# Ordering 28 experts by their row counts: sorting keys with the eight-maximum instruction

## The chip, the cores and the metric

The kernel runs on one core of a Trainium2 chip. The metric is device time in microseconds (us) of one execution of the whole program; a lower time is better. Engines are named as in the profile: PE is TensorE (PEld its weight loads), DVE is VectorE, ACT is ScalarE, POOL is GpSimd, SP is the sync engine, which issues the large transfers from HBM.

## What is computed

One decoder block over 512 rows of 1024 values: a mixer (retention heads and differential attention heads, merged by gates, one output projection), then a mixture of 32 experts, then a final normalisation. The part that matters here is the mixture:

```python
gp = softmax(h @ w_rg + b_rg);  g_top, g_idx = top_k(gp, 1)
el = (h @ w_re + b_re) of the chosen group of 8
e_val, e_idx = top_k(el, 2)
weights = g_top * softmax(e_val);  expert = g_idx * 8 + e_idx
y[expert] = (silu(x @ w1[e]) * (x @ w3[e])) @ w2[e]
out = sum over the two experts of weights * y
```

Every row has two experts, and how many rows an expert has depends on the data. Each expert has three weight matrices of 2 MB each, all of which are read from HBM.

## The kernel before, in words

The program first does the mixer, then the router (which ends in the counts of rows of each expert, the tile `cnts`), then the experts. The experts' stage takes the experts in units of 128 row slots (`BLOCKS`, in the order `UNITS`). The first four experts (`NFIX`) are taken by number: units 0 and 1 are experts 0 and 1, then 2 and 3. The other 28 are taken by place in a list sorted by number of rows, since an expert with many rows gets more slots than one with few. The list, `order`, holds the expert's number at each place. The inverse, `place`, holds each expert's place; the gathers of rows use it through `pcode`, and `block_list` uses it to list rows that found no slot.

Weights come through `load_in` (gate and up matrices, eight transfers of 512 KB, line 662) and `load_down` (four transfers, line 670), all issued by SP in program order. Each goes into a buffer of a ring of 36, so a transfer waits on SP until the matmuls that read the buffer's last contents are through; whatever stands behind it on SP waits too. For an expert that is taken from the list, SP first reads the expert's number from `order` into a register (line 1373) and waits for it there.

At the end of the router, lines 1150 to 1164, the order of the instructions on every engine is the program's own (`manual_schedule`). ACT copies the counts (line 1153). DVE then works out the last chunk's slot codes and one-hot matrix, the row factors (`factors`, lines 993 and 995) and, after PE's products, the second half of the gathered rows (`scaled`, line 1010). `turn` transposes the gathered rows on PE and scales them into `xT`, the first four blocks on ACT (line 1038) and the last four on DVE (line 1035). After that come `exps` and `weights`, short DVE instructions that make each row's weight in `aux`. Then expert 0's matmuls (`Expert.unit`, line 1222) run.

In the experts' stage only PE's order is fixed by the program. The other engines' instructions are placed by a planner, which estimates when each can start. `run_experts` calls `order_experts` by its hook after expert 0's matmuls have been put down: the whole ordering is DVE work that stands there among the products of the activations (line 1227), the one-hot matrices of the next gather (lines 976 and 978) and the short instructions of `sides` (lines 1043 to 1051). `order_experts` makes keys, compares all 28 with all 28 in a table of 784 values per partition and sums its rows to `place` (lines 1292 and 1295). From `place` it makes `order` with a second table: compare with the numbers of the places (line 1298), multiply by the experts' numbers (line 1300), sum (line 1301), convert (line 1302). The rest moves the row codes to the new places (lines 1304 to 1315). `block_list` (lines 1322 to 1361) is some fifty further short DVE instructions.

`Gather.unit` (lines 1012 to 1023) makes the next unit's rows between the matmuls of an expert; its products on PE (line 1000) wait for the one-hot chunk of line 978.

Of the kernel before, what the change touches and what calls it, by code (L numbers as in the profile page):

```python
# [7 lines left out]
F32 = mybir.dt.float32  # L8
F32R = mybir.dt.float32r
BF16 = mybir.dt.bfloat16  # L10
I32 = mybir.dt.int32
U32 = mybir.dt.uint32
AF = mybir.ActivationFunctionType
ALU = mybir.AluOpType
AX = mybir.AxisListType
# [3 lines left out]
P = 128  # L19
# [5 lines left out]
NEXP = 32  # L25
# [4 lines left out]
NFIX = 4  # L30
# [89 lines left out]
def block_kernel(tc, a, out):  # L120
    nc = tc.nc
    vec, act, pe, pool = nc.vector, nc.scalar, nc.tensor, nc.gpsimd

    def left(name, bufs=1):
        return open_pool(tc, name, bufs, side="left", reuse_waits="tile")

    def right(name, bufs=1):
        return open_pool(tc, name, bufs, side="right", reuse_waits="tile")
# [3 lines left out]
    cp, cp_close = left("consts")  # L132
# [185 lines left out]
    def run(it):  # L318
        for _ in it:
            pass  # L320

    def merged(*its):
        its = list(its)
        while its:
            its = [it for it in its if next(it, 0) is None]
            yield
# [13 lines left out]
    with tc.manual_schedule():  # L340
# [54 lines left out]
        for j in range(NJ):  # L395
            n, k0 = START_STEPS[j], k0s[j]
# [31 lines left out]
            order = [(0, b, m) for m in range(3) for b in range(4)] + [(1, b, m) for b in range(3) for m in range(3)]  # L428
# [337 lines left out]
    rt, rt_close = right("router")  # L766
# [27 lines left out]
    iotae = cst[:, C_IOTAE:C_IOTAE + NEXP]  # L794
# [12 lines left out]
    def router_bias():  # L807
        ps = pm.tile([P, S], F32, name="ps")
        pe.matmul(ps[:, 0:36], onef, wsum, start=True, stop=True)
        vec.tensor_add(br, br, ps[:, 0:36])  # L810
# [5 lines left out]
    vec.memset(gl, -3e38)  # L816
    cnts = cp.tile([P, NEXP], F32, name="cnts")
    efs = cp.tile([P, NT, 2], F32, name="efs")
    Ms = [rt.tile([P, NEXP], BF16, name=f"M{i}") for i in range(NT)]
    for i in range(NT):  # L820
        vec.tensor_scalar(aux[:, i, 0:1], cst[:, C_PIDX:C_PIDX + 1], float(i * P), None, op0=ALU.add)
# [7 lines left out]
    def sm_(name, cols=1, dt=F32):  # L829
        keep = {"s1": 4, "gs": 4, "den": 4, "wx": 4, "g8": 3, "e8": 3, "oh": 3, "rj": 1, "el": 1}  # L830
        return rt.tile([P, cols], dt, name=name, bufs=keep.get(name, 2))

    class Chunk:
# [115 lines left out]
        def weights(self):  # L949
            i = self.i  # L950
            vec.tensor_copy(aux[:, i, 1:2], efs[:, i, 0:1])
            vec.tensor_mul(self.den, self.den, self.gs)
            vec.reciprocal(self.den, self.den)
            vec.tensor_scalar(self.wx, self.wx, self.den, None, op0=ALU.mult)
            vec.tensor_copy(aux[:, i, 2:4], self.wx)
            vec.tensor_sub(aux[:, i, 4:6], self.wx, aux[:, i, 2:4].bitcast(F32))

    def g_tile():
        return gp.tile([P, NT, P], F32R, name="G")

    def row_tile():
        return gp.tile([P, KD, P], F32, name="xT")
# [122 lines left out]
    with tc.manual_schedule():  # L1085
        ch = [Chunk(i) for i in range(NT)]
        g0 = Gather(dcode, aux, cst[:, C_CBASE:C_CBASE + 2 * CAP], cst[:, C_ESLOT:C_ESLOT + 1],
                    lambda: pm.tile([P, S], F32, name="ps"), lambda: pm.tile([P, S], F32, name="ps"), g_tile())
        for i in range(NT):
            c, b, d = ch[i], ch[i - 1] if i else None, ch[i - 2] if i > 1 else None  # L1090
            c.project(0)
            c.project(1)
            if b:
                b.turn(1)
                b.logits(0)
                b.logits(1)
            c.turn(0)
            if d:
                d.count()
                run(d.codes())  # L1100
                d.exps()
            c.square(0)
            c.split(0)
            if i == NT - 1:
                c.logits(0)
            c.project(2)
            if b:
                b.turn_logits()
                b.split(1)
            if d:  # L1110
                d.factor()
                run(g0.build_chunk(d.i))
            c.project(3)
            if i == 0:
                router_bias()
            c.residual(2 if i == NT - 1 else 1)
            if i < NT - 1:
                c.square(1)
            if b:
                run(b.choose())  # L1120
        pss = [pj.tile([P, S], F32, name="pj") for _ in range(2)]
        b, c = ch[NT - 2:]

        def gather(i, *nhs):
            for nh in nhs:
                g0.product(pss[nh], i, nh)
                if nh:
                    g0.side_product(i, FACTOR)

        gather(0, 0, 1)  # L1130
        c.turn(1)
        c.square(1)
        c.logits(1)
        c.split(1)
        b.count()
        c.turn_logits()
        gather(1, 0, 1)

        def rest():
            yield from b.codes()  # L1140
            yield from g0.build_chunk(b.i)
            b.factor()
            yield
            c.factor()
            yield
        run(merged(c.choose(), rest()))
        gather(b.i, 0)
        c.count()
        gather(b.i, 1)
        pc = pm.tile([P, S], F32, name="ps")  # L1150
        for q in range(NT):
            pe.matmul(pc[:, 0:NEXP], oneb, Ms[q], start=(q == 0), stop=(q == NT - 1))
        act.copy(cnts, pc[:, 0:NEXP])
        run(c.codes())
        run(g0.build_chunk(c.i))
        g0.side_product(c.i, FACTOR)
        for nh in range(2):
            g0.product(pss[nh], c.i, nh)
            if nh == 0:
                g0.factors()  # L1160
            g0.scaled(pss[nh], nh)
        g0.turn(row_tile())
        b.exps()
        c.exps()
        act.activation(lame, ones.to_broadcast([P, 2]), AF.Silu)
        for c in ch:
            c.weights()
# [10 lines left out]
    mk, mk_close = right("moe")  # L1178
# [100 lines left out]


    place = mk.tile([P, NEXP], F32, name="place")
    order = mk.tile([P, NEXP], I32, name="order")
    pcode = cp.tile([P, 2, NT], F32, name="pcode")
    paux = cp.tile([P, NT, 8], F32R, name="paux")

    def order_experts():
        n = NEXP - NFIX
        key = mk.tile([P, NEXP], F32, name="key")
        vec.scalar_tensor_tensor(key, cnts, -float(NEXP), iotae, op0=ALU.mult, op1=ALU.add)
        t = mk.tile([P, D], F32, name="yt", bufs=1)  # L1290
        c = t[:, 0:n * n].rearrange("p (a b) -> p a b", a=n)
        vec.tensor_tensor(c, key[:, NFIX:, None].to_broadcast([P, n, n]),
                          key[:, None, NFIX:].to_broadcast([P, n, n]), op=ALU.is_gt)
        vec.tensor_copy(place[:, 0:NFIX], iotae[:, 0:NFIX])
        vec.reduce_sum(place[:, NFIX:], c, axis=AX.X)
        vec.tensor_scalar(place[:, NFIX:], place[:, NFIX:], float(NFIX), None, op0=ALU.add)

        vec.tensor_tensor(c, place[:, None, NFIX:].to_broadcast([P, n, n]),
                          iotae[:, NFIX:, None].to_broadcast([P, n, n]), op=ALU.is_equal)
        vec.tensor_mul(c, c, iotae[:, None, NFIX:].to_broadcast([P, n, n]))  # L1300
        vec.reduce_sum(key[:, NFIX:], c, axis=AX.X)
        vec.tensor_copy(order[:, NFIX:], key[:, NFIX:])

        vec.tensor_sub(key, place, iotae)
        c = t[:, 0:2 * NT * NEXP].rearrange("p (a b) -> p a b", a=2 * NT)
        ef = efs.rearrange("p i k -> p (i k)")
        vec.tensor_tensor(c, ef[:, :, None].to_broadcast([P, 2 * NT, NEXP]),
                          iotae[:, None, :].to_broadcast([P, 2 * NT, NEXP]), op=ALU.is_equal)
        vec.tensor_mul(c, c, key[:, None, :].to_broadcast([P, 2 * NT, NEXP]))
        mv = mk.tile([P, NT, 2], F32, name="mv")  # L1310
        vec.reduce_sum(mv.rearrange("p i k -> p (i k)"), c, axis=AX.X)
        for k in range(2):
            vec.scalar_tensor_tensor(pcode[:, k, :], mv[:, :, k], 512.0, dcode[:, k, :], op0=ALU.mult, op1=ALU.add)
        vec.tensor_copy(paux, aux.bitcast(F32))
        vec.tensor_add(paux[:, :, 1], efs[:, :, 0], mv[:, :, 0])
# [172 lines left out]
    def hook(e):  # L1488
        if e == 0:
            order_experts()  # L1490
        if e == 6:
            block_list()
# [59 lines left out]
```

## Time and profile before

| what | value |
|---|---|
| time, median of 3 runs (lowest, highest) | 1133.92 us (1133.46, 1135.08) |
| the profiled execution: its own time, its span | 1135.46 us, 1133.7 us |
| mean granted TensorE clock in it | 0.989 of full speed |
| busy share of the span: PE, PEld, DVE, ACT, POOL | 95%, 59%, 55%, 30%, 7% |
| moved by DMA | 284.02 MB, mean 251 GB/s |
| experts' stage (first expert's matmuls to last weights landed) | about 640 to 1115 us of the span |

The busy shares are means over stages with different limits: in the mixer PE leads, in the experts' stage the weights' transfers occupy the DMA engines nearly all the time. A change in the middle of the program is therefore read from the stretch it lies in. A "form" such as 128x784 gives partitions and elements per partition.

### The profile page before, as it was taken

To read this page: it belongs to the slowest core of one execution; us is meant where nothing else is said; L and a number is where in the kernel's file an instruction comes from. 1 tells how busy PE (TensorE), PEld (TensorE's weight loads), DVE (VectorE), ACT (ScalarE), POOL (GpSimd) and SP (SyncE) were. 2 spreads that over 40 slices of the span, in tenths; PEclk is the share of its full clock that TensorE was granted. 3 is DMA by queue.
4 is the path that set the end of the run, shared out by engine and by line. 5 is a ranking of instruction groups with operands and counts; after the bars stand their busy time and mean duration, and the time that the engine had idled before them with its cause. 6 is when DMAs were issued, how large, how long until landed. Compare 5 with 4: busy or idle time off the path is not lost.

```text
span 1133.7 us, 15015 instructions
## 1 busy us (share of the span) xinstructions
PE 1071.7 (95%) x5178; PEld 665.0 (59%) x5178; DVE 622.2 (55%) x1443; ACT 338.4 (30%) x701; POOL 79.0 (7%) x106
## 2 busy tenths in 40 slices
PE   5999999999999999999999899999999999999885
PEld 3777778778788776788877444444432443234222
DVE  3468667644445765655775765755442553244244
ACT  4553233333343534444334211111111110111123
POOL 1031000000021111000013100000000000000001
PEclk9999999999999999999999999999999999999998
DMA  9945645622323221244286899999999999999994
GB/s 317 274 149 186 222 132 185 204 76 81 105 82 105 75 74 39 75 151 146 91 278 235 302 373 391 391 400 393 391 392 400 392 391 391 400 393 394 389 397 159
DMA packets 139889, 284.02 MB, mean 251 GB/s; under 512 B 10977, under 2 KB 34585, under 8 KB 139681
## 3 DMA queue, kind: packets, MB, share of 16 engines
q1 hardware_dynamic: 136656, 281.29, 68.6%
q10 hardware_dynamic: 3152, 1.73, 0.6%
q8 instruction: 42, 0.69, 0.3%
q14 instruction: 39, 0.31, 0.1%
HBM read 280.88 MB, written 2.11 MB: 250 GB/s over the span
## 4 chain that ended last, share of the span: by engine, by line
PE 67%; DMA 19%; DVE 7%; ACT 2%; issue 2%; POOL 1%; SPq 0%; ACTq 0%; DVEq 0%; POOLq 0%
PE pj L209 31%; PE gu L1222 12%; DMA ew<-in_w_exp_up_dram 9%; DMA ew<-in_w_exp_down_dram 5%; PE py L1242 5%; PE pa L1000 4%; PE pa L1269 4%; DMA wa<-in_w_ada_dram 3%; PE pj L391 2%; PE ps L485 2%; PE ps L695 1%; DMA wst<-in_w_in_dram 1%; DVE acc L462 1%; PE ps L391 1%; DVE qk L448 1%
## 5 line engine op out<-in xcount | busy, mean ns | idle before, releaser
L1222 PE MATMUL gu<-ew,xT 128*64 128x512 f32 (+1 forms) x1088 | 222.4, 601 | 12.6 <-DMA ew<-in_w_exp_gate_dram 8.4
L209 PE MATMUL pj<-ew,whi 128*128 128x512 f32 x512 | 168.2, 410 | 0.0
L164 DVE TENSOR_TENSOR wlo<-wst,whi 128x1024 fp32r<-128x1024 f32 x79 | 100.0, 1267 | 87.0 <-ACT whi L163 79.5
L209 PE MATMUL pj<-whi,ew 128*128 128x512 f32 x384 | 131.0, 409 | 2.8 <-DVE v L480 2.8
L1222 PEld LDWEIGHTS gu<-ew,xT 128*64 128x64 f32 (+1 forms) x1088 | 54.4, 123 | 133.7 <-issue 88.4
L1242 PE MATMUL py<-ew,hTm 128*64 128x512 f32 (+1 forms) x544 | 116.1, 599 | 6.9 <-DMA ew<-in_w_exp_down_dram 6.8
L163 ACT CAST whi<-wst 128x1024 fp32r<-128x1024 f32 x79 | 82.8, 1050 | 130.3 <-PE pj L209 122.1
L209 PEld LDWEIGHTS pj<-ew,whi 128*128 128x128 f32 x512 | 94.2, 190 | 23.6 <-issue 2.8
L209 PE MATMUL pj<-ew,wlo 128*128 128x512 f32 x256 | 101.8, 398 | 0.0
L209 PEld LDWEIGHTS pj<-whi,ew 128*128 128x128 f32 x384 | 73.6, 192 | 22.8 <-DVE v L480 3.2
L1275 DVE TENSOR_TENSOR x<-x,pa 128x512 f32<-128x512 f32 x96 | 59.5, 682 | 47.4 <-PE pa L1269 47.4
L1247 DVE SCALAR_TENSOR_TENSOR yt<-py,ws,g2b 64x512 f32<-64x512 f32 x52 | 39.0, 750 | 72.3 <-PE py L1242 71.7
L1242 PEld LDWEIGHTS py<-ew,hTm 128*64 128x64 f32 (+1 forms) x544 | 27.9, 123 | 84.1 <-issue 44.3
L209 PE MATMUL pj<-wlo,ew 128*128 128x512 f32 x192 | 76.9, 401 | 0.0
L1227 DVE TENSOR_TENSOR sg<-sg,gu 64x512 f32<-64x512 f32 x26 | 17.9, 690 | 97.1 <-ACT sg L1226 96.3
L209 PEld LDWEIGHTS pj<-ew,wlo 128*128 128x128 f32 x256 | 48.5, 189 | 11.7
L1269 PE MATMUL pa<-xs,ct 128*128 128x512 f32 x196 | 52.8, 409 | 0.1
L209 PE MATMUL pj<-xhi,whi 128*128 128x512 f32 x128 | 51.7, 404 | 0.0
L1269 PEld LDWEIGHTS pa<-xs,ct 128*128 128x128 f32 x196 | 35.0, 188 | 26.9 <-issue 12.4
L209 PE MATMUL pj<-xhi,wlo 128*128 128x512 f32 x128 | 50.7, 396 | 0.0
L209 PE MATMUL pj<-xlo,whi 128*128 128x512 f32 x128 | 50.7, 396 | 0.0
L1263 ACT CAST xs<-yt 128x512 fp32r<-128x512 f32 x25 | 15.5, 619 | 112.9 <-DVE yt L1247 68.1
(364 smaller groups left out, 1548.1 us busy)
## 6 DMA issues: line engine op xcount, KB each, us to landing
ew<-in_w_exp_gate_dram SPq DMA_DIRECT2D x128, 512.0 KB, 10.6
ew<-in_w_exp_up_dram SPq DMA_DIRECT2D x128, 512.0 KB, 10.7
ew<-in_w_exp_down_dram SPq DMA_DIRECT2D x128, 512.0 KB, 10.4
wa<-in_w_ada_dram SPq DMA_DIRECT2D x44, 512.0 KB, 4.8
wst<-in_w_in_dram SPq DMA_DIRECT2D x20, 1024.0 KB, 5.6
wst<-in_w_in_dram SPq DMA_DIRECT2D x16, 512.0 KB, 4.3
wst<-in_w_ret_o_dram SPq DMA_DIRECT2D x4, 1024.0 KB, 4.9
wst<-in_w_diff_o_dram SPq DMA_DIRECT2D x4, 1024.0 KB
```

The costliest lines, as they stand in the source:

```text
L163: act.copy(hi, src[:, off:off + 2, :])
L164: vec.tensor_sub(lo, src[:, off:off + 2, :], hi.bitcast(F32))
L209: pe.matmul(bank, l, r, start=(k == 0 and j == 0), stop=(k == KD - 1 and j == 2))
L391: pe.matmul(bank, w, (hhi, hhi, hlo)[m][:, k, :], start=(k == 0 and m == 0), stop=(k == KD - 1 and m == 2))
L485: pe.matmul(out, l[a_], r[b_], start=start and j == 0, stop=stop and j == 2)
L1000: pe.matmul(ps, self.G[:, i, :], hx[:, i, ns], start=(i == 0 and j == 0), stop=(i == NT - 1 and j == 1))
L1222: pe.matmul(self.gu[r:r + n, :], self.g.xT[:, k, c:c + n], w[name, k // 2][:, k % 2, :], start=(k == 0), stop=(k == KD - 1))
L1227: vec.tensor_mul(self.sg, self.sg, self.gu[64:P, :])
L1242: pe.matmul(py[r:r + n, :], self.hT[:, k, n * q:n * q + n], w[k][:, nh, :], start=(k == 0), stop=(k == 3))
L1247: vec.scalar_tensor_tensor(yt[r, ns], py[64 * nh:64 * nh + 64, :], self.g.w[r], g2b[r, ns], op0=ALU.mult, op1=ALU.mult)
L1269: pe.matmul(po, self.ct[:, i * P:(i + 1) * P], self.ys[nh][:, j, :], start=start and j == 0, stop=(j == 1))
L1275: vec.tensor_add(x1[:, i, ns], x1[:, i, ns], po)
```

## The change

The list `order` is no longer made from `place` in `order_experts`. A generator `sort_experts` makes it at the end of the router. It forms the key 32 times the count plus the expert's number, takes the eight largest keys with `vec.max`, replaces these by -1 with `vec.match_replace`, and repeats until 32 have been taken (28 are real). The keys are converted to integers and their lowest five bits, the expert's number, are kept. Ten instructions are put down: four after `factors`, the other six after the second `scaled`, ahead of `turn`. `place` is still made by the first table, with the key's sign turned so that both agree; between two experts with the same count, the one with the larger number now comes first, where it was the smaller. `order` moves from the experts' pool to that of the constants, and the new small tiles lie in the router's pool.

```diff
+    order = cp.tile([P, NEXP], I32, name="order")
...
+    def sort_experts():
+
+        key = [rt.tile([P, NEXP], F32, name="key", bufs=2)[:, NFIX:] for _ in range(2)]
+        srt = sm_("srt", NEXP)
+        vec.scalar_tensor_tensor(key[0], cnts[:, NFIX:], float(NEXP), iotae[:, NFIX:], op0=ALU.mult, op1=ALU.add)
+        yield
+        for j in range(NEXP // 8):
+            top = srt[:, 8 * j:8 * j + 8]
+            vec.max(top, key[j % 2])
+            yield
+            if j < NEXP // 8 - 1:
+                vec.match_replace(key[(j + 1) % 2], top, key[j % 2], -1.0)
+                yield
+        ints = sm_("ints", NEXP, I32)
+        vec.tensor_copy(ints[:, NFIX:], srt[:, 0:NEXP - NFIX])
+        yield
+        vec.tensor_single_scalar(order[:, NFIX:], ints[:, NFIX:], NEXP - 1, op=ALU.bitwise_and)
+        yield
...
+        sorting = sort_experts()
         for nh in range(2):
             g0.product(pss[nh], c.i, nh)
             if nh == 0:
                 g0.factors()
+                for _ in range(4):
+                    next(sorting)
             g0.scaled(pss[nh], nh)
+        run(sorting)
         g0.turn(row_tile())
...
-    order = mk.tile([P, NEXP], I32, name="order")
...
-        vec.scalar_tensor_tensor(key, cnts, -float(NEXP), iotae, op0=ALU.mult, op1=ALU.add)
+        vec.scalar_tensor_tensor(key, cnts, float(NEXP), iotae, op0=ALU.mult, op1=ALU.add)
...
-        vec.tensor_tensor(c, key[:, NFIX:, None].to_broadcast([P, n, n]),
-                          key[:, None, NFIX:].to_broadcast([P, n, n]), op=ALU.is_gt)
+        vec.tensor_tensor(c, key[:, None, NFIX:].to_broadcast([P, n, n]),
+                          key[:, NFIX:, None].to_broadcast([P, n, n]), op=ALU.is_gt)
...
-        vec.tensor_tensor(c, place[:, None, NFIX:].to_broadcast([P, n, n]),
-                          iotae[:, NFIX:, None].to_broadcast([P, n, n]), op=ALU.is_equal)
-        vec.tensor_mul(c, c, iotae[:, None, NFIX:].to_broadcast([P, n, n]))
-        vec.reduce_sum(key[:, NFIX:], c, axis=AX.X)
-        vec.tensor_copy(order[:, NFIX:], key[:, NFIX:])
```

## Rows read from the trace of the kernel before

**Rows 1.** The page, part 2: DMA busy tenths in 40 slices of the span.
```profile
DMA  9945645622323221244286899999999999999994
```

**Rows 2.** Waits of PE, 800 to 1110 us: total us, times, longest.
```profile
PE gu L1222 <- DMA ew<-in_w_exp_gate_dram: 8.4, 9, 1.7
```

**Rows 3.** Windows: busy us of PE, PEld, DVE, ACT, POOL; clock, DMA share, GB/s.
```profile
646.00:648.00 2.00, 2.00 (x14) 0.89 (x12) 2.00 (x5) 0.59 (x1) 0.00 (x0) 1.00 0.80 288
648.00:671.00 23.00, 21.42 (x104) 9.07 (x102) 18.45 (x83) 3.53 (x8) 0.00 (x0) 1.00 1.00 370
654.00:656.00 2.00, 1.37 (x7) 0.90 (x6) 2.00 (x13) 0.00 (x0) 0.00 (x0) 1.00 0.97 312
660.00:664.00 4.00, 4.00 (x23) 1.80 (x24) 3.52 (x15) 2.00 (x5) 0.00 (x0) 1.00 0.96 326
667.00:670.00 3.00, 3.00 (x16) 0.84 (x13) 1.06 (x2) 0.00 (x0) 0.00 (x0) 1.00 0.89 330
700.00:1050.00 350.00, 341.06 (x1746) 139.08 (x1744) 164.23 (x393) 52.09 (x108) 0.00 (x0) 1.00 1.04 394
```

**Rows 4.** SP's longest wait for the list, and SP's timeline of issues around it.
```profile
SPq L1373 <- DVE key L1304: 4.4, 1, 4.4
...
645.27 2.83 SPq L670 DMA_DIRECT2D ew<-in_w_exp_down_dram  x4
653.14 0.41 SPq L662 DMA_DIRECT2D ew<-in_w_exp_gate_dram  x1
...
658.03 0.37 SPq L662 DMA_DIRECT2D ew<-in_w_exp_gate_dram  x1
...
661.93 0.37 SPq L662 DMA_DIRECT2D ew<-in_w_exp_gate_dram  x1
```

**Rows 5.** Chain of 640 to 672 us in order of time: start, us, what.
```profile
648.15 0.98 DVE yt L1298
...
649.30 0.88 DVE yt L1300
...
650.90 0.88 DVE key L1301
...
651.98 0.09 DVE order L1302
```

**Rows 6.** Waits of PE, 648 to 662 us.
```profile
PE pt L1232 <- DVE ax L1043: 0.9, 1, 0.9
PE pa L1000 <- DVE G L978: 0.6, 2, 0.3
```

**Rows 7.** Timeline of DVE in the router's choice: start us, us, instruction.
```profile
629.29 0.20 DVE L906 MAX8 e<-el 128x8 f32<-128x32 f32 x1
...
629.52 0.09 DVE L909 MATCH_VALUE_LOAD ei<-e,el 128x8 f32 x1
629.60 0.18 DVE L909 FIND_INDEX8 ei<-e,el 128x8 uint32<-128x32 f32 x1
...
629.82 0.17 DVE L911 CAST efs<-ei 128x2 f32<-128x2 uint32 x1
```

**Rows 8.** Timeline where the sort will stand, and what follows it.
```profile
638.48 0.75 DVE L1010 TENSOR_SCALAR xs<-pj,sl 128x512 f32<-128x512 f32 x1 [1.54 <-PE pj L1000]
...
639.87 7.09 PE L1222 MATMUL gu<-ew,xT 128*64 128x512 f32 x32
639.98 1.36 DVE L1035 TENSOR_SCALAR xT<-ps,A,sh 128x128 f32<-128x128 f32 x4 [0.75 <-PE ps L1031]
...
645.39 0.16 DVE L956 TENSOR_TENSOR aux<-wx,aux 128x2 fp32r<-128x2 f32 x1
...
646.89 0.61 PE L990 MATMUL pt<-aux,G 128*128 128x6 f32 x4
647.43 3.65 PE L1222 MATMUL gu<-ew,xT 128*64 128x512 f32 x16
```

**Rows 9.** Timeline of DVE: four of the short instructions of the row list.
```profile
658.09 0.87 DVE L1334 SCALAR_TENSOR_TENSOR nb<-key,nb 128x32 f32<-128x32 f32 x4
```

## The prediction

> **What bounds the kernel now.** I read the 40 slices first, to see which resource is full in the experts' stage, then the waits of PE near the end, then a table of windows, and last the waits, the chain and the timelines of the 30 us in which the change lies. The slices show the DMA engines full from about two thirds of the span to the last slice but one [rows 1]. From 800 us on PE waits for weights, 8.4 us for those of the gate matrices alone [rows 2]. So the end is set by the stream of weights: it moves 394 GB/s from 700 to 1050 us [rows 3], and the program ends a fixed tail after the last transfer. Nothing that DVE or PE gains in this stage counts by itself; what counts is how much of the stream has gone through by the time from which it never pauses again, some 670 us.
>
> Before that it does pause. From 648 to 671 us it moves 370 GB/s [rows 3]: 23 x (1 - 370/394) = **1.40 us** of full stream lost. The dips are at 654 (2 x (1 - 312/394) = 0.42 us), at 660 (4 x (1 - 326/394) = 0.69) and at 667 (3 x (1 - 330/394) = 0.49) [rows 3]; together 1.60, of which the stretches between give 0.2 back by running a little above the mean. SP's rows tell what each pause waited for. SP put down four transfers by 648.1, then stood 4.4 us at the list, and issued the first transfer of a listed expert at 653.14 [rows 4], when the four, 2.1 MB or 5.3 us of the stream, were nearly through: the first dip. The next issues, at 658.03 and 661.93 [rows 4], come when expert 1's matmuls free the buffers, so these dips follow PE. And PE in this stretch waits for DVE: 0.9 us at the transposes of line 1232 and 0.6 us at the gather of line 1000 [rows 6].
>
> **The change part by part.** *Removed:* the second table. Its four instructions fill 0.98 + 0.88 + 0.88 + 0.09 = 2.83 us of a chain that is DVE's alone there [rows 5]. The first table stays, with its operands exchanged and a sign turned, at the same cost.
>
> *Added:* one key instruction, four MAX8, three replacements (each a load of the eight values and a pass), a conversion and a mask. MAX8 over 32 values is in the trace: the instruction that depends on it starts 0.23 us later (629.29 to 629.52) [rows 7]. MATCH_REPLACE8 is not. The nearest row is the search for eight values, which has the same load in front: 0.30 us from the load to the dependent conversion (629.52 to 629.82) [rows 7]. I take 0.30; it can hardly be under the pass alone, 0.18 us, and as upper end I take 0.49, that is a MAX8 more with its wait, 0.19 longer. Key, conversion and mask I put at 0.20 each, the step from that conversion's class of instruction.
>
> The first four steps are 0.20 + 0.23 + 0.30 + 0.23 = 0.96 us. They stand where DVE idles 1.54 us ahead of line 1010 [rows 8], so they cost nothing; at the upper price they take 1.15 and still fit. If they ran over 1.54 us, the second half of the rows, its transposes and expert 0 would be late by the excess. The other six are 0.30 + 0.23 + 0.30 + 0.23 + 0.20 + 0.20 = 1.46 us (1.22 to 1.84 by the ends). In front of line 1035 DVE idles 0.75 us [rows 8], so 0.71 us (0.47 to 1.09) push line 1035 and all of DVE behind it. Who waits for that? PE needs the fifth block of `xT` half way through expert 0's 32 matmul records, at 639.87 + 7.09/2 = 643.4 us, and would have it near 641.1: 2.3 us spare. The last of `aux` comes at 645.55 + 0.71 = 646.26, and PE takes it at 646.89 [rows 8]: 0.6 us spare. ACT, with its own part of `xT`, is not touched. So the push stays on DVE.
>
> *Net on DVE's chain at 652 us:* -2.83 + 0.71 = **-2.1 us**. PE's two waits, 0.9 and 0.6, end that much earlier and vanish: PE gains 1.5 us and is then bound by its own matmuls.
>
> *The list on SP:* ready near 640.7 (638.48 + 0.75 + 1.46) where it was at 652.1. SP, free at 648.1, doesn't stop, but the first listed transfers need expert 1's first buffers. Its 16 records of 3.65 us begin at 647.43 [rows 8] and cover four of the eight blocks; one pair of transfers holds two blocks, so pairs of buffers come free at 649.3 and 651.1. The four transfers are put down some 3.5 us earlier than before, behind work that lasts to about 654: the first dip goes. SP's reading of the register stays on SP, and no transfer is moved past another.
>
> *The other dips:* with the first gone, the stream stands 0.42 us further, so to close the second the issues must come 0.42 + 0.69 = 1.11 us earlier, to close the third 1.60. PE's 1.5 us gives the second whole and the third nearly. The sort's tiles come last in the router's pool, where the experts' own small tiles lie later and not the weights' buffers, so I count no new wait on SP.
>
> *Sum:* the stream gains 1.4 us, and so does the end. Bounds: at least the first dip, 0.4; at most all of 1.40 and the pause at 646 to 648 too, 2 x (1 - 288/394) = 0.54 [rows 3], so 1.9. I take 1.4, since the spare times above are all positive. The profiled execution took 1135.46 us, of which its span is 1133.7, and 1134.06 would be left. It stands 1.54 us above the median of the runs, 1133.92; against that the forecast is **1132.5 us**. Some 0.2%, or 2.3 us, is what a measurement of this kernel can tell from no change, and the forecast lies inside.
>
> One row bears on the trade itself: 784 values took up to 0.98 us [rows 5], 32 values 0.20 [rows 7], so a short instruction is nearly all fixed cost, and the change puts ten in place of four. The Trainium skill speaks against that trade (VectorE: DVE Perf Modes, "The TRN2 errata" and "Rules for kernel authors"): every instruction pays a fixed extra latency, small tiles pay it each time, and one should minimise the count of instructions. By that rule the change is rival B below, with 1133.2 us where the rows give 1132.5; the trace agrees on the fixed cost, but shows idle time under more than half of the new instructions.
>
> **The rivals.** *B, the short instructions eat the relief.* If the idle stretches do not hold the sort, all ten steps, 2.4 us, stand on DVE's chain and the net is -0.4 us: PE's waits shrink by 0.4, the first dip goes, the second closes in part. Gain about 0.7 us, 1133.2. Against it: the 1.54 and 0.75 us idle are in the rows, and the first is needed for two thirds only.
>
> *C, the pauses come back.* The first listed transfers go early, but the buffers behind them come no earlier, since PE finds another wait on DVE or for weights; the dip moves instead of closing: 1133.9. For it: three of the four causes are buffers, not the list. Against it: PE's waits in this stretch name DVE alone [rows 6].
>
> *D, more than the dips.* If the stream after the list also runs closer and DVE's whole 2.83 us reach it, the time is 1131.1. Against it: the stream has only 1.4 us to give from 648 us, 1.9 from 646.
>
> *E, slower: the planner's new order.* DVE's order from 645 us on is planned. With the long instructions gone the plan may pull the short ones of `block_list` forward, ahead of the one-hot chunks of line 978 and the product of line 1227. Four such took 0.87 us [rows 9], and there are some fifty. It decides from ten on: 10 x 0.22 = 2.2 us cancels the relief. With all of the first 25 ahead, 5.4 us, PE is 3.3 us later than now, the buffers with it, and less the first dip the end comes 2.9 us later: 1136.8. Against it: before, the plan kept most of them behind the chunks.
>
> **How the numbers follow.** Forecast 0.58; B 0.12; C 0.08; D 0.15; E 0.07. Faster by over 0.2% is D and a little scatter, 0.17; within 0.2% is the forecast, B and C, 0.75; slower is E, 0.08 with scatter. The range leaves out E and a third of D: 1130.9 to 1135.0, with half a us on each side for the scatter of the runs.
>
> **What would show it.** In the changed profile: no wait of SP at line 1373 near 648, the first listed gate transfer issued near 649.3, no PE wait at line 1232 or 1000 before 657, MATCH_REPLACE8 near 0.2 us, line 1035 starting near 640.7, and a window of 648 to 671 at some 394 GB/s with the 700 to 1050 rate unchanged. Wrong would be: expert 0's matmuls starting after 639.9, DVE placing line 1334 or 1340 before line 978, a dip of the stream that is only later, or an end that moves by more than the dips held.

## The result: 1118.2 us, and the profile after

The changed kernel takes 1118.24 us (median of 4 runs, 1117.64 to 1120.26), the kernel before 1134.5 us beside it; the ratio is 0.9859 with a 95% interval of 0.9834 to 0.9885. That is 16 us where 1.4 were forecast, far outside the range. The profiled execution took 1117.88 us, its span is 1116.1.

First the slices of the page, which answer to [rows 1], and the page's line of rates under them.

```profile
DMA  9845645622323211244275799999999999999994
GB/s 334 267 151 189 222 141 184 207 77 77 113 76 114 76 59 56 75 152 151 76 259 227 286 394 399 397 414 402 402 404 405 410 398 405 410 400 409 397 408 158
```

The DMA engines are as full as before in the experts' stage, but the rates there read 394 to 414 GB/s. The windows say the same with one number. They are of the changed kernel, with the columns of [rows 3]; the first is the start of the program, the second answers to 648 to 671 of before (expert 0's matmuls begin 5.1 us earlier, so it is shifted by 5), the third to fifth to the three dips, the last to the same 350 us as before.

```profile
0.00:50.00 50.00, 37.80 (x202) 26.74 (x203) 19.76 (x41) 25.34 (x38) 3.71 (x12) 0.97 0.97 317
643.00:666.00 23.00, 23.00 (x112) 9.77 (x112) 16.02 (x78) 3.64 (x9) 0.00 (x0) 1.00 1.03 404
649.00:651.00 2.00, 2.00 (x12) 1.13 (x10) 1.73 (x11) 0.00 (x0) 0.00 (x0) 1.00 1.02 404
655.00:659.00 4.00, 4.00 (x24) 1.91 (x24) 3.71 (x12) 2.10 (x5) 0.00 (x0) 1.00 1.05 405
662.00:665.00 3.00, 3.00 (x18) 1.03 (x16) 0.00 (x0) 0.37 (x1) 0.00 (x0) 1.00 1.02 405
700.00:1050.00 350.00, 342.00 (x1786) 139.75 (x1782) 166.95 (x399) 52.48 (x109) 0.00 (x0) 1.00 1.04 404
```

Two things are to be seen. The dips are gone: all three windows move what the long one moves, and PE is busy for all of the 23 us. And the long window, hundreds of microseconds behind the last changed instruction, moves 404 GB/s where it moved 394 [rows 3], at the same DMA share, 1.04. The engines are no busier; each byte takes less of their time. The start of the program is faster too: in the kernel before, its first 50 us moved 309 GB/s.

```profile
0.00:50.00 50.00, 37.11 (x200) 26.11 (x201) 19.94 (x41) 25.91 (x38) 3.78 (x12) 0.97 0.99 309
```

Where the 17.6 us between the two spans lie can be read from two marks, the start of expert 0's matmuls and the issue that follows the last weights. Before, these are at 639.87 [rows 8] and 1105.78, after at 634.75 and 1088.14.

```profile
1105.78 0.34 SPq L1439 DMA_DIRECT2D ew<-in_norm_final_dram  x1
```

```profile
634.75 7.62 PE L1246 MATMUL gu<-ew,xT 128*64 128x512 f32 x32
...
1088.14 0.34 SPq L1456 DMA_DIRECT2D ew<-in_norm_final_dram  x1
```

So 5.1 us come ahead of the experts, 12.5 between the marks (465.9 to 453.4), and none in the tail (27.9 and 28.0). At the two rates, 465.9 us would become 465.9 x 394/404 = 454.4, which is 11.5 of the 12.5; about 1 is left for the dips.

The sort itself stands on DVE as the prediction has it. This is the timeline of DVE in the changed kernel, from `factors` to `turn`.

```profile
631.26 0.18 DVE L963 SCALAR_TENSOR_TENSOR key<-cnts,cst 128x28 f32<-128x28 f32 x1
631.47 0.19 DVE L967 MAX8 srt<-key 128x8 f32<-128x28 f32 x1
631.70 0.09 DVE L970 MATCH_VALUE_LOAD key<-srt,key 128x8 f32 x1
631.77 0.17 DVE L970 MATCH_REPLACE8 key<-srt,key 128x28 f32<-128x28 f32 x1
631.98 0.19 DVE L967 MAX8 srt<-key 128x8 f32<-128x28 f32 x1
632.90 0.75 DVE L1030 TENSOR_SCALAR xs<-pj,sl 128x512 f32<-128x512 f32 x1 [0.73 <-PE pj L1020]
...
634.58 0.18 DVE L973 CAST ints<-srt 128x28 int32<-128x28 f32 x1
634.79 0.18 DVE L975 TENSOR_SCALAR order<-ints 128x28 int32<-128x28 int32 x1
634.88 1.36 DVE L1055 TENSOR_SCALAR xT<-ps,A,sh 128x128 f32<-128x128 f32 x4
```

The first four steps fill 0.91 us of the idle stretch and leave 0.73 idle behind them. A replacement with its load takes 0.28 us to the next MAX8 (631.70 to 631.98), for which 0.30 was taken. Line 1055 starts 1.23 us after line 1030 ends, 0.48 more than before. PE's two waits of [rows 6] do not stand in the changed kernel at all, and SP's wait at the list, 4.4 us in [rows 4], is down to 0.5:

```profile
SPq L1390 <- DVE yt L1326: 0.5, 1, 0.5
```

### The profile page after: what moved, and what is told of

Read it like the earlier page. It is cut to its first block, busy times and chain, and to the rows that moved or that the text cites. A ratio compares the mean times of both kernels' runs of the same rounds, so it can differ in the third digit from the quotient of the medians.

```text
span 1116.1 us, 15022 instructions
## 1 busy us (share of the span) xinstructions
PE 1063.5 (95%) x5178; PEld 663.2 (59%) x5178; DVE 621.4 (56%) x1452; ACT 337.9 (30%) x701; POOL 78.9 (7%) x106
## 4 chain that ended last, share of the span: by engine, by line
PE 70%; DMA 19%; DVE 5%; issue 2%; ACT 2%; POOL 1%; ACTq 0%; SPq 0%; DVEq 0%; POOLq 0%
PE pj L209 33%; PE gu L1246 12%; DMA ew<-in_w_exp_up_dram 9%; DMA ew<-in_w_exp_down_dram 6%; PE py L1266 5%; PE pa L1293 4%; PE pa L1020 3%; DMA wa<-in_w_ada_dram 3%; PE pj L391 3%; PE ps L485 2%; PE ps L695 1%; DVE acc L462 1%; PE ps L391 1%; DVE qk L448 1%; PE ps L374 1%
## 5 line engine op out<-in xcount | busy, mean ns | idle before, releaser
L1246 PE MATMUL gu<-ew,xT 128*64 128x512 f32 (+1 forms) x1088 | 217.6, 602 | 9.3 <-DMA ew<-in_w_exp_gate_dram 6.5
L163 ACT CAST whi<-wst 128x1024 fp32r<-128x1024 f32 x79 | 82.8, 1050 | 128.3 <-PE pj L209 120.2
L1293 PEld LDWEIGHTS pa<-xs,ct 128*128 128x128 f32 x196 | 34.9, 188 | 26.8 <-issue 11.5
```

The source lines that it names most:

```text
L163: act.copy(hi, src[:, off:off + 2, :])
L1246: pe.matmul(self.gu[r:r + n, :], self.g.xT[:, k, c:c + n], w[name, k // 2][:, k % 2, :], start=(k == 0), stop=(k == KD - 1))
L1293: pe.matmul(po, self.ct[:, i * P:(i + 1) * P], self.ys[nh][:, j, :], start=start and j == 0, stop=(j == 1))
```

## The experiments

After the result two theories stood. **Sort**: the sort and the early list bring it, by something in the stream that the prediction missed. **Addresses**: the new 128-byte tile `order` lies in the constants, at the bottom of the left side, so every left tile above it moved by 128 bytes, the buffers of the weights among them. The memory maps of the two compiled programs show it (start of each group in bytes of a partition, and the rest modulo 256; the ring's 36 buffers are hT 8, mw1 7, mw4 3 on the left, mw2 10 and mw3 8 on the right):

```
            hT           mw1            mw4            mw2            mw3
before     3968 (128)   103040 (128)   131712 (128)   188384 (224)   155616 (224)
after      4096 (0)     103168 (0)     131840 (0)     188384 (224)   155616 (224)
```

A third, **chip**, was that the two profiles simply come from different sessions. Ratios below are to runs of the kernel before on the same chip, with 95% intervals.

**1. The kernel before, again.** No edit.

> The kernel before, unchanged, with a profile from the same chip as the three kernels beside it. Chip theory (the 16 us lie in the chip or the session on which each profile was taken): its stream from 700 to 1050 us runs at some 404 GB/s and it takes 1118 us. Theories that put the cause in the program (sort, addresses): 394 GB/s and 1134 us, as in the profile of before.

Measured: 1132.99 us, ratio 0.9989 (0.9975 to 1.0004). Stream of this run:

```profile
700.00:1050.00 350.00, 341.54 (x1746) 139.11 (x1746) 165.51 (x396) 53.07 (x110) 0.00 (x0) 1.00 1.04 394
```

**2. The changed kernel, again.** No edit.

> The changed kernel, unchanged, on the same chip. Chip theory: same time as the kernel before less the 1.4 us of the dips, ratio 0.998 to 1.000. Theories in the program: 1118 us, ratio 0.986, with 404 GB/s in the stream.

Measured: 1119.21 us, ratio 0.9868 (0.9848 to 0.9889), stream 404 GB/s. With run 1 the chip theory falls.

**3. 128 unused bytes, no sort.**

```diff
     efs = cp.tile([P, NT, 2], F32, name="efs")
+    pad = cp.tile([P, NEXP], I32, name="pad")
+    vec.memset(pad, 0)
```

> The kernel before, without the sort, with one unused tile of 128 bytes per partition in the constants, so that the weights' buffers on the left side (hT, mw1, mw4) and all tiles above the constants lie 128 bytes higher, as in the changed kernel. Address theory: most of the gain comes without any sort, 1119 to 1121 us, stream at some 404 GB/s. Sort theory: no gain, 1134 us at 394 GB/s. Chip theory: the same as the kernel before beside it.

Measured: 1120.96 us, ratio 0.9891 (0.9866 to 0.9917). The stream:

```profile
700.00:1050.00 350.00, 342.87 (x1792) 140.22 (x1788) 167.44 (x399) 53.06 (x110) 0.00 (x0) 1.00 1.04 404
```

The kernel before, with one tile that nobody reads, gains 12 to 14 us. The sort theory falls for all but the 1.75 us between this run and run 2, and the intervals of the two overlap.

**4. The sort, with the list in mw1.** Only mw4 above it moves.

```diff
-    order = cp.tile([P, NEXP], I32, name="order")
+    order = mw1.tile([P, NEXP], I32, name="order")
```

> The changed kernel with the sorted list in the pool mw1 in place of the constants: the sort is as changed, but all tiles under mw4 lie where they lay before; only the three buffers of mw4 are 128 bytes higher. Address theory: the gain is lost but for the dips, 1132 to 1133 us at 394 GB/s. Sort theory: the whole gain stays, 1118 us.

Measured: 1129.32 us, ratio 0.9958 (0.9938 to 0.9978), more than the dips and much less than the whole: between what the two theories had expected. The stream:

```profile
700.00:1050.00 350.00, 342.61 (x1766) 139.23 (x1761) 166.89 (x399) 52.43 (x109) 0.00 (x0) 1.00 1.04 396
```

Three of 36 buffers moved and the rate rose by 2 GB/s; 18 moved and it rose by 10. This run also holds its own control. A packet is one record of the DMA queue. Those of the gate and up matrices are of 2 KB; put in order after 680 us and counted back from the last weights, they can be given to the ring's buffers. The mean time of one is

```
buffers in     hT 86.9   mw1 88.4 to 88.5   mw4 84.9   mw2 88.2   mw3 87.8   ns
```

In the kernel before it is 88.1 to 88.4 ns in every group; in the changed kernel 84.1 to 84.8 on the left and 86.7 to 87.1 on the right. The count is good to some three transfers only, so a group next to a faster one (hT comes after mw4) reads between the two, and in run 6 mw4, which stays off the multiples there, reads 84.3 ns like mw3 ahead of it.

**5. The changed kernel, 128 bytes further.** The left is 256 bytes higher than before, at 128 past a multiple of 256 again.

```diff
     order = cp.tile([P, NEXP], I32, name="order")
+    pad = cp.tile([P, NEXP], I32, name="pad")
+    vec.memset(pad, 0)
```

> The changed kernel with 128 bytes more of an unused tile in the constants: all left tiles lie 256 bytes higher than in the kernel before, so their buffers start again at 128 past a multiple of 256. If what counts is a start at a multiple of 256 bytes, the stream falls back to 394 GB/s and only the sort's own gain is left: ratio to the kernel before near 0.9985 (1.4 to 1.8 us of 1134). If any shift away from the old place had done it (banks, neighbours), it stays near 1118 us and 404 GB/s.

Measured: 1132.34 us, ratio 0.9990 (0.9977 to 1.0003); the stream:

```profile
700.00:1050.00 350.00, 340.70 (x1740) 138.67 (x1738) 165.94 (x397) 52.70 (x109) 0.00 (x0) 1.00 1.04 393
```

The gain is gone with the sort in place. It is not the place but the start modulo 256.

**6. The right side alone, no sort.**

```diff
+    edge, edge_close = right("edge")
+    vec.memset(edge.tile([P, 56], F32, name="edge"), 0.0)
     wp, wp_close = right("wts")
```

> The kernel before, no sort, left side as it was, with a pool of 224 bytes put ahead of all others on the right side, so that the other 18 of the 36 weight buffers (mw2, mw3) and the weight staging tiles of the mixer start at multiples of 256. Alignment theory: about the same gain as for the left side, 1120 to 1125 us, stream at some 403 GB/s. If the left side is special: 1134 us.

Measured: 1119.22 us, ratio 0.9874 (0.9851 to 0.9898), 404 GB/s. Eighteen other buffers, the same gain: nothing is special in the left side.

**7. Both sides, no sort.** The edit of 6, and the list's tile moved as in the change:

```diff
+    order = cp.tile([P, NEXP], I32, name="order")
...
-    order = mk.tile([P, NEXP], I32, name="order")
```

> The kernel before, no sort, with the list's tile moved to the constants (128 bytes, left side) and 224 bytes on the right: all 36 weight buffers start at multiples of 256. Alignment theory: the two gains add, stream at 411 to 414 GB/s, 1106 to 1113 us. If something else limits the stream at 404: 1118 to 1121 us.

Measured: 1109.91 us, ratio 0.9793 (0.9765 to 0.9821). The stream reaches 409 GB/s, less than the 411 to 414 expected:

```profile
700.00:1050.00 350.00, 341.50 (x1798) 139.87 (x1796) 168.05 (x400) 53.01 (x110) 0.00 (x0) 1.00 1.04 409
```

**8. Both sides and the sort.** The change, the edit of 6, and the integers made in place:

```diff
-        ints = sm_("ints", NEXP, I32)
-        vec.tensor_copy(ints[:, NFIX:], srt[:, 0:NEXP - NFIX])
+        vec.tensor_copy(order[:, NFIX:], srt[:, 0:NEXP - NFIX])
         yield
-        vec.tensor_single_scalar(order[:, NFIX:], ints[:, NFIX:], NEXP - 1, op=ALU.bitwise_and)
+        vec.tensor_single_scalar(order[:, NFIX:], order[:, NFIX:], NEXP - 1, op=ALU.bitwise_and)
```

> The changed kernel with 224 bytes on the right as well (the sort's integers are made in the list's own tile, to make room): all 36 buffers at multiples of 256 and the sort. Alignment theory and a sort that gives its own gain: 1.4 to 1.8 us under the kernel without the sort beside it, 1104 to 1111 us. If the sort's gain comes from addresses alone: the same time as the one without it.

Measured: 1106.89 us, ratio 0.9763 (0.9740 to 0.9786). It is the fastest version, some 11 us under the changed kernel and 26 under the one before. By the medians the sort adds 3.0 us to run 7's gain; the intervals of the two overlap.

**9 and 10. Which part of the sort works.** Both start from run 5, so the addresses are the old ones. In both the second table runs as before, into a list of its own, `order2`; in 9 SP reads the sort's list, in 10 the table's.

```diff
+    order2 = mk.tile([P, NEXP], I32, name="order2")
...
+        vec.tensor_tensor(c, place[:, None, NFIX:].to_broadcast([P, n, n]),
+                          iotae[:, NFIX:, None].to_broadcast([P, n, n]), op=ALU.is_equal)
+        vec.tensor_mul(c, c, iotae[:, None, NFIX:].to_broadcast([P, n, n]))
+        vec.reduce_sum(key[:, NFIX:], c, axis=AX.X)
+        vec.tensor_copy(order2[:, NFIX:], key[:, NFIX:])
...
-        return (lambda: gather_unit(b)), [half and [(lambda e=e: fixed(e)) if e < NFIX else listed(order, e)
+        return (lambda: gather_unit(b)), [half and [(lambda e=e: fixed(e)) if e < NFIX else listed(order2, e)
```

The last two lines are in run 10 alone.

> The changed kernel at the old alignment (256 bytes higher), with the second table's four DVE instructions put back, their result unused: the list is early, DVE keeps its 2.8 us. If SP's wait for the list made the dips: SP does not stop and the stream loses little between 648 and 671 us, as without the table. If PE's wait for DVE made them, as the prediction has it for the later two: the first dip is closed, PE still waits 0.9 and 0.6 us or more at the transposes and the gather, and some 1 us is lost in the stream. Time within 2 us of the kernel before in both cases.

> The same, but SP reads the list that the second table makes; the sort runs and its list is unused. DVE has both: SP stands 4.4 to 5.1 us at the list, the dips are as in the kernel before or larger by the 0.7 us of the sort, and the time is that of the kernel before or up to 1 us more.

Measured: 1133.71 us, ratio 1.0007 (0.9992 to 1.0023), with the early list; 1133.65 us, 1.0007 (0.9991 to 1.0023), with the late one. The times can't tell them apart; the profiles can. First the run with the early list, PE's waits and a window of 23 us that begins 8 us after expert 0's matmuls (634.14 here), as 648 to 671 does in the kernel before:

```profile
PE pt L1258 <- DVE ax L1065: 1.4, 1, 1.4
PE pa L1022 <- DVE G L1000: 0.6, 2, 0.3
...
642.00:665.00 23.00, 20.95 (x102) 8.83 (x98) 19.20 (x84) 3.16 (x7) 0.00 (x0) 1.00 0.97 363
```

Then SP's wait at the list and the same window in the run with the late list (expert 0 from 636.27), where PE's waits are the same two:

```profile
SPq L1398 <- DVE key L1329: 4.9, 1, 4.9
...
644.00:667.00 23.00, 20.95 (x100) 8.78 (x98) 19.33 (x84) 3.24 (x8) 0.00 (x0) 1.00 0.98 358
```

And in run 5, where the table is gone (expert 0 from 637.70):

```profile
646.00:669.00 23.00, 23.00 (x112) 9.74 (x110) 15.98 (x77) 3.53 (x8) 0.00 (x0) 1.00 1.04 396
```

SP stands 4.9 us in the late one and has no such wait in the early one, and yet the stream moves 358 and 363 GB/s: against the 394 of the long window in both, 2.10 and 1.81 us are lost. In these windows the early list by itself buys 0.3 us, and 0.1 to 0.5 when both are moved by 1 us. Taking the table off DVE takes PE's waits away, 2.0 us with the sort in front (PE is busy 20.95 of 23 us in both, 23.00 without the table), and with them the dips.

**11. 64 bytes further.** The left starts at 64 past a multiple of 256.

```diff
     order = cp.tile([P, NEXP], I32, name="order")
+    pad = cp.tile([P, 16], I32, name="pad")
+    vec.memset(pad, 0)
```

> The changed kernel with 64 bytes more of an unused tile in the constants: the left buffers start 64 past a multiple of 256 (0 in the changed kernel, 128 in the one before). If every start off a multiple of 256 costs the same, as one more piece of a packet would: 394 GB/s and 1132 to 1133 us. If the cost grew with the offset: 398 to 400 GB/s.

Measured: 1132.86 us, ratio 0.9997 (0.9982 to 1.0011); the stream:

```profile
700.00:1050.00 350.00, 341.06 (x1738) 138.62 (x1736) 165.35 (x396) 52.95 (x110) 0.00 (x0) 1.00 1.04 393
```

64 costs what 128 costs.

## Why the prediction was wrong

**The step that failed** is the treatment of the moved tile, in the part on the other dips: "The sort's tiles come last in the router's pool, where the experts' own small tiles lie later and not the weights' buffers, so I count no new wait on SP." I asked where the new tiles lie and who must wait for their bytes, and let the rate of the stream stand: the bound of 1.9 us and the sign to look for, "the 700 to 1050 rate unchanged", both rest on 394 GB/s. `order` was named as moved to the constants and then had no price. But the constants lie under everything on the left, and half of the stream's destinations moved from 128 to 0 modulo 256. Runs 3 and 7 show what that is worth without the sort, 1.1% for half of the buffers and 2.1% for all; runs 5 and 11 show that the sort without it has next to nothing.

Most of the gain that the forecast had not is in the stream, 11.5 us by its two rates. The 5.1 us ahead of the experts are less sure. The first 50 us move 306 to 311 GB/s in the seven profiles in which at most mw4 starts at multiples of 256, 312 to 320 in the four with one side there, and 319 and 321 in the two with both. But the start of expert 0's matmuls scatters: 634.1 to 639.9 us, 633.1 to 635.6, and 629.2 and 630.4. So the first loads gain from addresses too, yet how much of the 5.1 us is the scatter of one execution I can't say.

The traces show a cost by the packet. Between 680 and 1060 us a packet of 2 KB takes 84.4 to 84.6 ns in the mean with all buffers at multiples of 256 (runs 7 and 8) and 88.1 to 88.3 with none (before and runs 1, 5, 9, 10, 11); one of 4 KB, as the down matrices have them, takes 159.5 and 163.6 to 163.7. That is some 4 ns more for either size. A rule that bears on this was to be had, and the prediction should have put a price on it. The Trainium skill (DMA: Bandwidth & Descriptors, "How a descriptor splits into AXI transactions") says that an aligned descriptor goes as pieces of 256 bytes, and that where one does not start at a multiple of 256, its first piece starts at the multiple below. By that, an estimate for 2 KB is nine pieces for eight. It also counts the bytes in front of the start as lost, by which the cost would grow with the offset. The section speaks of reads; here the source in HBM stayed and the destination moved. The runs would fit one more piece and not a cost that grows: 393 GB/s at 64 and 393 to 394 at 128 on the left. But the 4 ns are less than the 10.6 that an eighth of 84.5 would be, and no run shows that a piece is the cause.

**What held.** The stream sets the end: most of the change shows between two marks of it, and the tail behind it is the same. DVE's part held in size: steps of 0.28 for 0.30 us, 0.91 us for 0.96 in the first gap, line 1055 pushed by 0.48 for 0.71, PE's waits gone. The sort's own gain was put at 1.4 us. Three pairs of equal alignment give 1.75 us (runs 2 and 3), 3.0 (8 and 7) and 1.1 (run 5 by its ratio, interval -0.3 to 2.6), and run 11, of the same kind as run 5, 0.3 by its ratio. By the times the runs can't fix it closer than 0 to 3. The profiles can. In the 23 us that begin 8 us after the start of expert 0's matmuls, the five without the sort (before and runs 1, 3, 6, 7) move 369 to 377 GB/s, which is 1.0 to 2.0 us lost against the long window of each, and PE waits for DVE in all five. The six with the sort and without the table (after and runs 2, 4, 5, 8, 11) lose 0.3 us at most, and PE waits for DVE in none. So the size fits the forecast.

**What was wrong inside it.** "The four transfers are put down some 3.5 us earlier than before, behind work that lasts to about 654: the first dip goes." Run 9 does just that, with SP not stopping at the list, and still loses 1.81 us in the window where run 10 loses 2.10. What rival C said of the whole change is true of this part: the third listed pair is issued 18.6 us after expert 0's start in both runs, and 16.5 in run 5, with PE's 2.0 us of waits between them, so with the early list alone the next buffers come no earlier and the pause comes later. By these profiles the 1.4 us came almost wholly through PE, by DVE's relief, which the prediction had as the second of two causes. One price was also misread: a MAX8 more with its wait is 0.23 us by [rows 7], so the upper end of a replacement is 0.53, not 0.49; nothing turned on it, since it measured 0.28.

**The rivals.** One sign of being wrong came, an end that moves by more than the dips held. D was the nearest by sign, but its mechanism, more of DVE's 2.83 us reaching the end, is not what happened. B did not come: the idle stretches held the sort. E did not come: the one-hot chunks of line 998 were planned in time, and PE waits for none. None of the five said that the change does something beside what it says, and such a rival was there to be had in one line of the diff, the tile that changes its pool.

## What to carry to other kernels

When a change adds, drops or moves a tile, work out which addresses shift, and whether a stream that sets the end writes to them: here 128 bytes at the bottom of memory were worth several times the change that brought them. Start the buffers of large transfers at multiples of 256 bytes (394 GB/s off them here, 409 to 410 on them), and check it in the memory map, since a pool of small tiles underneath undoes it silently. And before crediting a change with its gain, run it once with its side effect alone (an unused tile of the same size) and once with the side effect cancelled.

## What the runs showed of the hardware

The rate of this stream of 512 KB transfers, in 2 and 4 KB packets, depends on where they start in a partition: 393 to 394 GB/s with none of the 36 buffers at a multiple of 256 bytes, 396 with three, 404 with eighteen, on either side, and 409 to 410 with all. Left starts at 64 and at 128 past a multiple cost the same, 393 and 393 to 394, and moving the right side from 224 to 0 gave the same 404 as moving the left from 128. The DMA engines read as equally busy, share 1.04, in all of them, so the share doesn't show this; only GB/s does. The second half of the buffers brought 5 to 6 GB/s where the first brought 10. The mean 2 KB packet shows the same, 88.2 ns before, 85.7 in the changed kernel, 84.6 in run 7; why it is less I did not find.
